# One decoder layer on one Trainium2 core: the mixer's groups reordered and taken off GpSimd, part of its low weights made earlier

## The chip, the cores and the metric

The kernel runs on one of the eight cores of a Trainium2 chip. A core has TensorE (PE in the profile; its weight loads are shown as PEld), VectorE (DVE), ScalarE (ACT), GpSimd (POOL), a queue engine for transfers (SyncE, SP) and 16 DMA engines. The metric is device time in microseconds (us). Before the change the median of three runs is 2429.63 us (2427.08 to 2433.99). A measurement of this kernel tells about 0.3%, some 7 us, from no change.

## The reference

The reference is one inference step of a hybrid decoder layer on 264 columns: 256 tokens of one prompt and 8 samples of one token each. All is float32.

```python
h += 0.5 * norm(swiglu_1(norm(h)))                      # 2048 -> 5632 -> 2048
u  = norm(h);  proj = u @ w_in                          # 2048 -> 10288
glu_a, glu_b, z, xBC, dt = split(proj)                  # 1024, 1024, 3072, 5120, 48
v  = silu(layernorm(causal_conv31(glu_a * sigmoid(glu_b))))
x, B, C = silu(causal_conv4(xBC))                       # 48 heads of 64, 8 groups of state 128
y  = ssd(x, softplus(dt), a, B, C) ; y = norm_of_group(y * silu(z))
h += norm(concat(v, y) @ w_out)
h += 0.5 * norm(swiglu_2(norm(h)))
h += norm(sigmoid(norm(h) @ w_gate) * (p @ w_proj))
```

For the prompt, `ssd` works in two chunks of 128 tokens: products of C and B masked and weighted with decays exp(a_i - a_j), times x, and a state carried from the first chunk to the second. For each sample it is one step: state times exp(dt a) plus the product of x dt and B, and y is that state times C. New convolution buffers and states are returned too.

## The kernel before

Activations lie with 128 features on the partitions and 264 columns beside each other. Every matrix product is made in three passes over split numbers: a weight is w = hi + lo and an activation x = (x0, x1), and `mm3` (L248) issues hi x0 (L250), hi x1 (L251) and lo x0 (L252). So each 128x128 weight tile costs three matmuls of 264 columns. One column block of the input projection ("a unit") has 16 such tiles, 48 matmuls.

Weights come through `Weights.load` (L138). A unit of up to 16 tiles is read in halves of 8 tiles, 512 KB each, into `wraw` (L153); ACT rounds a half to `whi` (L154), and DVE subtracts to give `wlo` (L155). Each of the three has four buffers, and loading runs two units ahead. The tables `PLAN` and `IN_ORDER` (L47) fix the order of the units.

The stages are: first feed-forward (44 gate and up pairs and 16 down columns in three chunks; L366 `ffn`), a small projection of p, then `u` for the mixer, made k by k (L534: DVE and POOL add the residual, DVE scales, ACT and DVE split) while PE already runs the first four columns of the input projection over the k that are ready. Then come the other 77 columns. For each of eight groups the order is B, C, x0, in four groups a GLU pair, x1, x2, z0, z1, z2; `dt` comes first of all, and the last four GLU pairs at the end.

Behind each column DVE and ACT do the short convolution (`do_conv`, L629: ACT scales, DVE adds three shifted terms, ACT takes SiLU). After x0, `decays` (L696) reads the prefix sums from memory into `ab` and `ea`, and ACT takes exponentials. After x2, `ssd` (L717) transposes x and B on PE (L727, L728), forms the decayed C B products, states and y. For the samples it writes the group's B and C to memory (`d_bc`, L785), reads C back spread over all partitions (`cbc`, L787), reads the three states in halves (`h0`, L792), multiplies them on POOL and sums them on DVE (L794). The gate of a group (`gate`, L809) runs behind x0 of the next group: y times silu(z) on DVE, squares on ACT, two additions on POOL into `run`, a matmul with ones (L306) that sums over partitions, and a scaling.

All transfers are issued by SP in one queue, in order: an issue that waits holds back those behind it. The instruction order on every engine is fixed when the program is built, by a scheduler; line numbers L216, L219, L243 are the helpers `tt`, `stt` and `act`, so groups are told apart by tile names.

Of the kernel before, what the change touches and what calls it, by code (L numbers as in the profile page):

```python
# [19 lines left out]
P = 128  # L20
# [93 lines left out]

_COLS = {}
# [12 lines left out]
class Weights:  # L128
# [4 lines left out]
    def __init__(self, tc, pool, w):  # L133
        self.tc, self.pool, self.w = tc, pool, w
        self.at = 0
        self.done = []

    def load(self, between=()):  # L138
# [5 lines left out]
        with nullcontext() if between else tc.high_priority(offset=1000):  # L144
            for a in range(0, n, 8):
# [8 lines left out]
                nc.scalar.copy(hi, raw)  # L154
                nc.vector.tensor_tensor(out=lo, in0=raw, in1=hi.bitcast(F32), op=ALU.subtract)  # L155
# [13 lines left out]
def kernel(ctx: ExitStack, tc: tile.TileContext, a: dict):  # L169
# [77 lines left out]

    def mm3(acc, wt, x, first, last):  # L248
# [3 lines left out]
        return nc.tensor.matmul(acc, lo, x[:, 0, :], start=False, stop=last).ins  # L252
# [76 lines left out]
    ws = Weights(tc, wpool, a["w"])  # L329
# [26 lines left out]
    def gemm_one(xs, kts, nunits=1):  # L356
        acc = acc_tile()
# [126 lines left out]
    bg.append(hist_mod)  # L484

# [48 lines left out]
    for k in range(KD + 2):  # L534
# [4 lines left out]
        if k >= 2:  # L539
            t = tmp()  # L540
            stt(t, H(k - 2), V("mix_pre", k - 2), r, ALU.mult, ALU.mult)
            us.append(split(t))
    ectx.close()
# [27 lines left out]
    def do_dt(acc):  # L571
# [21 lines left out]
        nc.sync.dma_start(d_dt[1], dta[:, NP_:])  # L593
# [6 lines left out]
        act(eap, eap, AF.Exp)  # L600
        pt = ps_tile([P, 2, 2, NH])
        for c in range(2):
            for i, s in ((0, dt), (1, dta)):
                nc.tensor.transpose(pt[:, c, i, :], s[:, P * c : P * c + P], ident[:NH, :NH])
        nc.scalar.copy(tm, pt)
        pc = ps_tile([P, 2, 2, NH])
        for c in range(2):
            nc.tensor.matmul(pc[:, 0, c, :], tri, tm[:, c, 1, :], start=True, stop=True)
            nc.tensor.matmul(pc[:, 1, c, :], ones, tm[:, c, 1, :], start=True, stop=True)
        nc.scalar.copy(acs, pc[:, 0])  # L610
        tt(dte, pc[:, 1], acs, ALU.subtract)
        act(dte, dte, AF.Exp)
        act(cd, pc[:, 1, 1, :], AF.Exp)
        pf = ps_tile([P, 2, P])
        for c in range(2):
            nc.tensor.matmul(pf[:NH, c, :], tm[:, c, 1, :], tri, start=True, stop=True)
        cs = tmp()[:NH]
        nc.scalar.copy(cs[:, :NP_].rearrange("h (c l) -> h c l", c=2), pf[:NH])
        nc.sync.dma_start(d_cs, cs[:, :NP_])
# [76 lines left out]
    def decays(g):  # L696

        hs = slice(HPG * g, HPG * g + HPG)
        ab = []
        for c in range(2):  # L700
            t = mp.tile([P, HPG, P], F32, tag="ab", bufs=2, name=nm("ab"))
            nc.sync.dma_start(t, d_cs[hs, P * c : P * c + P].partition_broadcast(P))
            for h in range(HPG):
                i = HPG * g + h
                act(t[:, h, :], t[:, h, :], AF.Relu, bias=acs[:, c, i : i + 1], scale=-1.0)
            act(t, t, AF.Exp, scale=-1.0)
            ab.append(t)
# [6 lines left out]
        act(ea, ea, AF.Exp)  # L714
        return ab, ea

    def ssd(g, bf, cf, xt, ab, ea):  # L717
# [5 lines left out]
        for c in range(2):  # L723
# [11 lines left out]
            b = mp.tile([P, P], F32, tag="btm", bufs=1, name=nm("btm"))  # L735
            nc.scalar.copy(b, pt[:, 3, :])
            btm.append(b)
        pcb = ps_tile([P, 2, P])
        for c in range(2):
            cols = slice(P * c, P * c + P)  # L740
            nc.tensor.matmul(pcb[:, c, :], bf[:, cols], cf[:, cols], start=True, stop=True)

        for c in range(2):
            cb = mp.tile([P, P], F32, tag="cb", bufs=1, name=nm("cb"))
            tt(cb, pcb[:, c, :], tri, ALU.mult)
            tt(ab[c], ab[c], cb.unsqueeze(1).to_broadcast([P, HPG, P]), ALU.mult)

        states = []
        for c in range(2):
# [7 lines left out]
            else:  # L757
                tt(s, states[0], cd[:, hs].unsqueeze(2).to_broadcast([P, HPG, 64]), ALU.mult, nc.gpsimd)
# [18 lines left out]
        tt(y[:, :, P:NP_], y[:, :, P:NP_], ea, ALU.add)  # L777

        js = slice(3 * g, 3 * g + 3)
        pr = ps_tile([P, 2, P])  # L780
        nc.tensor.transpose(pr[:NS, 0, :], bf[:, NP_:], ident)
        nc.tensor.transpose(pr[:NS, 1, :], cf[:, NP_:], ident)
        rows = mp.tile([P, 2, P], F32, tag="rows", bufs=1, name=nm("rows"))
        nc.scalar.copy(rows[:NS], pr[:NS])
        nc.sync.dma_start(d_bc[g].rearrange("i b n -> b i n"), rows[:NS])  # L785
        cbc = mp.tile([P, NS, P], F32, tag="cbc", bufs=1, name=nm("cbc"))
        nc.sync.dma_start(cbc, d_bc[g, 1].partition_broadcast(P))  # L787
        ych = mp.tile([P, 3, NS], F32, tag="ych", bufs=1, name=nm("ych"))
# [375 lines left out]
```

## Time and profile before

| what | value |
|---|---|
| median of three runs | 2429.63 us |
| profiled execution | 2432.44 us, span 2430.7 us |
| PE busy | 2367.7 us, 97% |
| DVE, ACT, POOL busy | 1569.2, 1181.4, 298.4 us |
| first feed-forward, steady part (100 to 700 us) | PE busy throughout, 182 GB/s |
| `u` and first four columns | about 775 to 815 us |
| rest of the input projection with all of the mixer | about 815 to 1360 us |
| output projection | about 1360 to 1545 us |
| second feed-forward, last stage | about 1545 to 2320 us, to the end |

PE is the engine that the whole kernel is built around, so time is read as time in which PE is not busy, or runs at a lower granted clock, and from the list of what PE waited for in each stretch. A wait of another engine matters only where PE waits for its result.

### The profile page before, as it was taken

What the parts mean: (1) busy time and instruction counts of PE and PEld (TensorE: products, weight loads), DVE (VectorE), ACT (ScalarE), POOL (GpSimd) and SP (SyncE); (2) the same over time, 40 slices, a digit from 0 to 9 for tenths busy, and PEclk for the clock granted to TensorE, in tenths of its full rate; (3) what the DMA queues carried; (4) which work ended last, traced back from release to release, by engine and by line L of the source; (5) the groups of instructions that cost most, each with busy time, mean ns of one, the idle gap of its engine ahead of it and who ended that gap; (6) DMA issues with size and microseconds to landing.
All of it is one profiled execution on the core that took longest, in us unless ns stands there. A gap on an engine that the chain in (4) does not pass through costs nothing.

```text
span 2430.7 us, 47409 instructions
## 1 busy us (share of the span) xinstructions
PE 2367.7 (97%) x19448; PEld 2342.7 (96%) x19448; DVE 1569.2 (65%) x2333; ACT 1181.4 (49%) x1771; POOL 298.4 (12%) x295
## 2 busy tenths in 40 slices
PE   8999999999999889999999999999999999999988
PEld 8999999999999889999999999999999999999988
DVE  6554455545557858988798975766545565565585
ACT  6444444433456465665565545544444443344465
POOL 0400000000015212122122010101000000000103
PEclk9999999999999999999999999999999999999999
DMA  7655555555556666666666556476766776676553
GB/s 249 217 183 184 182 183 182 183 183 183 183 169 207 213 180 193 207 216 202 210 216 205 181 181 216 153 238 228 240 213 223 237 236 217 217 236 206 184 191 132
DMA packets 166250, 489.89 MB, mean 202 GB/s; under 512 B 25568, under 2 KB 42640, under 8 KB 166032
## 3 DMA queue, kind: packets, MB, share of 16 engines
q1 hardware_dynamic: 166032, 486.86, 62.0%
q8 instruction: 152, 2.49, 0.4%
q14 instruction: 66, 0.54, 0.1%
HBM read 465.65 MB, written 22.42 MB: 201 GB/s over the span
## 4 chain that ended last, share of the span: by engine, by line
PE 84%; DVE 6%; issue 3%; ACT 3%; DMA 2%; POOL 1%; SPq 0%; ACTq 0%; POOLq 0%; DVEq 0%
PE acc L250 27%; PE acc L251 27%; PE acc L252 27%; DVE wlo L155 2%; DVE y L219 1%; ACT whi L154 1%; PE ps L306 1%; DVE h L216 1%; DMA ab<-d_cs 1%; DMA cbc<-d_bc 1%; DVE ych L794 1%; PE ps L250 0%; ACT tmp L243 0%; DMA d_bc<-rows 0%; PE ps L251 0%
## 5 line engine op out<-in xcount | busy, mean ns | idle before, releaser
L252 PE MATMUL acc<-act,wlo 128*128 128x264 f32 x6224 | 1770.7, 285 | 4.3 <-DVE wlo L155 4.1
L251 PE MATMUL acc<-act,whi 128*128 128x264 f32 x6224 | 1756.6, 283 | 6.3 <-DVE act L216 6.2
L250 PE MATMUL acc<-act,whi 128*128 128x264 f32 x6224 | 1747.7, 283 | 3.4 <-DVE tmp L216 2.1
L155 DVE TENSOR_TENSOR wlo<-wraw,whi 128x1024 fp32r<-128x1024 f32 (+2 forms) x812 | 986.9, 1217 | 597.9 <-ACT whi L154 595.5
L154 ACT CAST whi<-wraw 128x1024 fp32r<-128x1024 f32 (+2 forms) x812 | 829.9, 1026 | 961.9 <-PE acc L251 717.3
L250 PEld LDWEIGHTS acc<-act,whi 128*128 128x128 f32 x6224 | 1175.5, 190 | 6.0 <-issue 2.1
L251 PEld LDWEIGHTS acc<-act,whi 128*128 128x128 f32 x6224 | 1169.2, 188 | 9.9 <-DVE act L216 7.9
L252 PEld LDWEIGHTS acc<-act,wlo 128*128 128x128 f32 x6224 | 1167.9, 188 | 8.3 <-DVE wlo L155 6.4
L216 POOL TENSOR_TENSOR run<-run,tmp 128x264 f32<-128x264 f32 x93 | 87.8, 944 | 962.9 <-ACT tmp L243 961.8
L216 POOL TENSOR_TENSOR s<-s,eap 128x1024 f32<-128x1024 f32 x24 | 48.8, 2035 | 630.4 <-DMA s<-in_hst 630.4
L219 DVE SCALAR_TENSOR_TENSOR y<-v,vec,y 128x251 f32<-128x251 f32 (+23 forms) x240 | 118.1, 512 | 1.2
L219 DVE SCALAR_TENSOR_TENSOR s<-bb,xds,s 128x128 f32<-128x128 f32 x192 | 52.7, 346 | 66.1 <-POOL s L216 66.1
L216 POOL TENSOR_TENSOR h<-h,cbc 128x512 f32<-128x512 f32 x48 | 73.6, 1553 | 166.0 <-DMA cbc<-d_bc 90.9
L258 ACT CAST act<-tmp 128x264 fp32r<-128x264 f32 x120 | 48.7, 410 | 69.9 <-DVE tmp L216 55.2
L216 DVE TENSOR_TENSOR tmp<-acc,rr 128x264 f32<-128x264 f32 x100 | 43.0, 430 | 51.0 <-PE acc L252 50.8
L216 DVE TENSOR_TENSOR tmp<-tmp,acc 128x264 f32<-128x264 f32 x86 | 36.7, 427 | 38.7 <-PE acc L252 38.6
L216 DVE TENSOR_TENSOR act<-tmp,act 128x264 fp32r<-128x264 f32 x120 | 56.1, 471 | 0.3
L243 ACT ACTIVATE tmp<-tmp 128x264 f32<-128x264 f32 x112 | 47.0, 420 | 8.7 <-DVE tmp L216 8.4
L243 ACT ACTIVATE tmp<-y 128x264 f32<-128x264 f32 x67 | 28.0, 425 | 44.1 <-DVE y L216 43.0
L216 DVE TENSOR_TENSOR y<-y,acc 128x264 f32<-128x264 f32 x80 | 34.0, 425 | 24.0 <-PE acc L252 24.0
L794 DVE TENSOR_REDUCE ych<-h 128x4 f32<-128x512 f32 x48 | 32.4, 678 | 17.5 <-POOL h L216 17.5
L250 PE MATMUL ps<-act,whi 128*128 128x264 f32 x96 | 28.4, 304 | 15.4 <-ACT whi L154 8.1
(165 smaller groups left out, 926.1 us busy)
## 6 DMA issues: line engine op xcount, KB each, us to landing
wraw<-in_w SPq DMA_DIRECT2D x756, 512.0 KB, 4.7
h<-in_hst SPq DMA_DIRECT2D x48, 256.0 KB, 3.9
s<-in_hst SPq DMA_DIRECT2D x24, 512.0 KB, 6.5
out_nss<-s SPq DMA_DIRECT2D x24, 512.0 KB, 3.0
wraw<-in_w SPq DMA_DIRECT2D x24, 384.0 KB, 4.1
wraw<-in_w SPq DMA_DIRECT2D x32, 256.0 KB, 3.9
ab<-d_cs SPq DMA_DIRECT2D x16, 384.0 KB, 5.1
cbc<-d_bc SPq DMA_DIRECT2D x8, 512.0 KB, 4.3
```

What stands on the lines that cost most here:

```text
L154: nc.scalar.copy(hi, raw)
L155: nc.vector.tensor_tensor(out=lo, in0=raw, in1=hi.bitcast(F32), op=ALU.subtract)
L216: return (eng or nc.vector).tensor_tensor(out=out, in0=in0, in1=in1, op=op)
L219: return nc.vector.scalar_tensor_tensor(out=out, in0=in0, scalar=scalar, in1=in1, op0=op0, op1=op1)
L243: i = nc.scalar.activation(out=out, in_=in_, func=func, bias=bias, scale=scale)
L250: nc.tensor.matmul(acc, hi, x[:, 0, :], start=first, stop=False)
L251: nc.tensor.matmul(acc, hi, x[:, 1, :], start=False, stop=False)
L252: return nc.tensor.matmul(acc, lo, x[:, 0, :], start=False, stop=last).ins
L258: nc.scalar.copy(t[:, 0, :], x)
L306: nc.tensor.matmul(p, ones, s, start=i == 0, stop=i == len(self.parts) - 1)
L794: nc.vector.tensor_reduce(out=ych[:, j, b : b + 4], in_=h0, op=ALU.add, axis=AX.X)
```

## The change

**Order.** `IN_ORDER` puts the three z columns of group 0 behind dt, so that the first four columns are dt, z0, z1, z2 instead of dt, B, C, x0. C of a group now comes behind x2 of the group before it (C of group 0 behind the z), and z of groups 1 to 7 behind that.

**Low weights.** Of the 81 units of the input projection, 30 (the first four and then every third) are staged: during the first feed-forward, behind every second column, one half is read (`sraw`), rounded on ACT (`shi`), subtracted in place on DVE and written to a new memory tensor `low`. In the mixer these units still read `wraw` and make `whi`, but `wlo` is read from `low`. That is 60 loads, casts, subtractions and stores more in the first feed-forward, 60 subtractions fewer and 60 loads of 512 KB more later.

**Mixer.** POOL has no work in the groups: the product of state and C is made on DVE, whole states (512 KB) at a time, the state's decay (`st`) and the gate's two additions also. The product with C moves from behind x2 to behind x0, x1 and x2 (x1, x2 and the next C in the first two groups). The gate is cut in two: `gate_begin` behind B of the next group, `gate_end` behind its x0. The prefix sums and the decays are loaded earlier and used behind x1, and `decay_cb` (the C B products with the decays) also behind x1. `do_dt` is cut in parts. The exponential of the samples' decay is taken before its way through memory.

```diff
@@ the column order of the mixer's input projection
     for g in range(GRP):
+        z = [("z", MT_Z + 3 * g + j) for j in range(3)]
+        if g == 0:
+            out.extend(z)
+            out.append(("C", MT_CM))
         out.append(("B", MT_BM + g))
-        out.append(("C", MT_CM + g))
         out.append(("x", MT_X + 3 * g))
         if g in GLU_IN:
             pair()
         out.extend(("x", MT_X + 3 * g + j) for j in (1, 2))
-        out.extend(("z", MT_Z + 3 * g + j) for j in range(3))
+        if g + 1 < GRP:
+            out.append(("C", MT_CM + g + 1))
+        if g:
+            out.extend(z)
...
+def _staged():
+    ins = [i for i, u in enumerate(PLAN) if u[0] == "in"]
+    return ins[:4] + ins[5::3]
+STAGED = _staged()
@@ class Weights
+    def stage(self, pool, s, a):
+        tc, nc = self.tc, self.tc.nc
+        cols = slice(8 * P * a, 8 * P * (a + 1))
+        raw = pool.tile([P, 8 * P], F32, tag="sraw", bufs=3, name=f"sraw{s}_{a}")
+        hi = pool.tile([P, 8 * P], F32R, tag="shi", bufs=1, name=f"shi{s}_{a}")
+        with tc.issue_after(self.dma.ins):
+            nc.sync.dma_start(raw, self.w[STAGED[s], :, cols])
+        nc.scalar.copy(hi, raw)
+        lo = raw.bitcast(F32R)
+        nc.vector.tensor_tensor(out=lo, in0=raw, in1=hi.bitcast(F32), op=ALU.subtract)
+        with tc.issue_after(self.dma.ins):
+            nc.sync.dma_start(self.low[s, :, cols], raw)
...
                 self.dma = nc.sync.dma_start(raw, src[:, a : a + m, :])
-                nc.scalar.copy(hi, raw)
-                nc.vector.tensor_tensor(out=lo, in0=raw, in1=hi.bitcast(F32), op=ALU.subtract)
+                self.hi = nc.scalar.copy(hi, raw).ins
+                if i in STAGED:
+                    low = self.low[STAGED.index(i), :, a * P : (a + m) * P]
+                    nc.sync.dma_start(lo.bitcast(F32), low.rearrange("p (n c) -> p n c", n=m))
+                else:
+                    self.lo = nc.vector.tensor_tensor(
+                        out=lo, in0=raw, in1=hi.bitcast(F32), op=ALU.subtract
+                    ).ins
@@ gemm_one, and the first feed-forward
+        paced[0] += 1
+        if stage and paced[0] % 2:
+            stage.popleft()()
...
+    for i in range(len(STAGED)):
+        for half in range(2):
+            stage.append(lambda i=i, half=half: ws.stage(ep, i, half))
@@ the samples' state products
+    def to_memory(g, i, t):
+        pr = ps_tile([P, P])
+        nc.tensor.transpose(pr[:NS], t[:, NP_:], ident)
+        rows = mp.tile([P, P], F32, tag="rows", bufs=1, name=nm("rows"))
+        nc.scalar.copy(rows[:NS], pr[:NS])
+        nc.sync.dma_start(d_bc[g, i], rows[:NS])
...
+    def load_state(g, j):
+        h0s[g, j] = mp.tile([P, NS, P], F32, tag="h0", bufs=2, name=nm("h0"))
+        with tc.issue_after(ws.dma.ins):
+            nc.sync.dma_start(h0s[g, j], a["hst"][3 * g + j])
+    def state_times_c(g, j):
...
+        with tc.issue_after(ws.lo):
+            tt(h0, h0, cbcs[g], ALU.mult)
+            nc.vector.tensor_reduce(out=ychs[g][:, j, :], in_=h0, op=ALU.add, axis=AX.X)
...
-        for j in range(3):
-            for b in range(0, NS, 4):
-                h0 = mp.tile([P, 4, P], F32, tag="h0", bufs=3, name=nm("h0"))
-                nc.sync.dma_start(h0, a["hst"][3 * g + j][:, b : b + 4, :])
-                tt(h0, h0, cbc[:, b : b + 4, :], ALU.mult, nc.gpsimd)
-                nc.vector.tensor_reduce(out=ych[:, j, b : b + 4], in_=h0, op=ALU.add, axis=AX.X)
@@ the states and the gate
-                tt(s, states[0], cd[:, hs].unsqueeze(2).to_broadcast([P, HPG, 64]), ALU.mult, nc.gpsimd)
+                tt(s, states[0], cd[:, hs].unsqueeze(2).to_broadcast([P, HPG, 64]), ALU.mult)
...
-    def gate(g, y, zs):
+    def gate_begin(g, y, zs):
         tt(y, y, zs, ALU.mult)
-        sq = SumSq(3, direct=0)
+        sq = SumSq(3, direct=0, eng=nc.vector)
         for j in range(3):
             sq.add(y[:, j, :])
+        return g, y, sq
+    def gate_end(g, y, sq):
         t = tmp()
-        rsqrt(t, sq.total(), eps1, 1.0 / 384)
+        rsqrt(t, sq.total(traced[0]), eps1, 1.0 / 384)
@@ the loop over the columns
         elif kind == "B":
...
+            if g:
+                gated.append(gate_begin(g - 1, y, zs))
+                load_sums(g)
...
+            else:
+                do_sums(dt, dta)
+                load_cbc(0)
+            load_state(g, 0)
+            load_state(g, 1)
         elif kind == "C":
...
+            to_memory(g, 1, bcs[g, 1])
+            if 1 <= g <= 2:
+                state_times_c(g - 1, 2)
+                ssd_samples(g - 1, bcs[g - 1, 0], bcs[g - 1, 1], xt, y)
         elif kind == "x":
...
+            if j == 1:
+                if g == 0:
+                    do_exps(dta)
+                ab, ea = decays(g)
             do_conv(acc, m - MT_X, xt[:, j, :])
+            late = 0 if g > 1 else 1
+            if j >= late:
+                state_times_c(g, j - late)
...
+                if g:
+                    gate_end(*gated.pop())
```

The built order shows the staging on SP, in the first feed-forward, where every row before was a load into `wraw`. `wraw_0` and `wraw_8` are the two halves of a unit; now the rows are:

```order
L183 DMA wraw_0_1523<-in_w 128x1024
L183 DMA wraw_8_1529<-in_w 128x1024
L161 DMA sraw_0_1586<-in_w 128x1024
L183 DMA wraw_0_1593<-in_w 128x1024
L183 DMA wraw_8_1599<-in_w 128x1024
L166 DMA low<-sraw_0_1586 128x1024
L183 DMA wraw_0_1659<-in_w 128x1024
```

Behind two halves of weights stands a load of `sraw`, and its store to `low` behind the next two.

While `u` is made, DVE's order has these rows before (`tmp<-h` and `act` are the scaled and the split k tile, `tmp<-y` the residual):

```order
L219 SCALAR_TENSOR_TENSOR tmp_9279<-h_87,vec,rr_9018 128x264
L216 TENSOR_TENSOR act_9265<-tmp_9263,act_9265 128x264
L155 TENSOR_TENSOR wlo_0_9406<-wraw_0_9404,whi_0_9405 128x1024
L216 TENSOR_TENSOR act_9273<-tmp_9271,act_9273 128x264
L219 SCALAR_TENSOR_TENSOR tmp_9287<-h_87,vec,rr_9018 128x264
L216 TENSOR_TENSOR tmp_9292<-y_3338,rr_9000 128x264
L219 SCALAR_TENSOR_TENSOR tmp_9295<-h_88,vec,rr_9018 128x264
L216 TENSOR_TENSOR act_9281<-tmp_9279,act_9281 128x264
L155 TENSOR_TENSOR wlo_8_9412<-wraw_8_9410,whi_8_9411 128x1024
```

and now, over the same k tiles:

```order
L255 SCALAR_TENSOR_TENSOR tmp_9632<-h_88,vec,rr_9379 128x264
L252 TENSOR_TENSOR tmp_9637<-y_3327,rr_9361 128x264
L252 TENSOR_TENSOR act_9626<-tmp_9624,act_9626 128x264
L255 SCALAR_TENSOR_TENSOR tmp_9640<-h_88,vec,rr_9379 128x264
L252 TENSOR_TENSOR act_9634<-tmp_9632,act_9634 128x264
L255 SCALAR_TENSOR_TENSOR tmp_9648<-h_88,vec,rr_9379 128x264
L252 TENSOR_TENSOR tmp_9653<-y_3459,rr_9361 128x264
L252 TENSOR_TENSOR act_9642<-tmp_9640,act_9642 128x264
```

The subtractions into `wlo` have gone from between the k tiles; the residual's rows and the rest stand as before.

For the gate, POOL's order in the mixer was, in each group, the last of the states times C (`h<-h,cbc`), the two additions into `run`, and the next group's `st`:

```order
L216 TENSOR_TENSOR h_562_10737<-h_562_10737,cbc_10718 128x512
L216 TENSOR_TENSOR h_563_10741<-h_563_10741,cbc_10718 128x512
L216 TENSOR_TENSOR run_11173<-run_11173,tmp_11175 128x264
L216 TENSOR_TENSOR run_11173<-run_11173,tmp_11178 128x264
L216 TENSOR_TENSOR st_11538<-st_11532,cd 128x384
```

Now DVE has all of these. Around the gate of a later group its order is:

```order
L252 TENSOR_TENSOR h_12589<-h_12589,h_12798 128x792
L189 TENSOR_TENSOR wlo_8_12935<-wraw_8_12933,whi_8_12934 128x1024
L255 SCALAR_TENSOR_TENSOR b_12987<-acc_12926,vec,b_12987 128x255
L252 TENSOR_TENSOR b_12987<-b_12987,shist 128x8
L252 TENSOR_TENSOR run_12996<-run_12996,tmp_12998 128x264
L255 SCALAR_TENSOR_TENSOR b_12987<-acc_12926,vec,b_12987 128x254
L252 TENSOR_TENSOR run_12996<-run_12996,tmp_13001 128x264
L252 TENSOR_TENSOR h_706_13011<-h_706_13011,cbc_12800 128x1024
L255 SCALAR_TENSOR_TENSOR b_12987<-acc_12926,vec,b_12987 128x253
```

The first row is y times silu(z), the `b` rows are the convolution of B of the next group, and the last-but-one is a whole state times C. Both additions stand ahead of the convolution of x0, where POOL made them behind x0; the matmul with ones that waits for them on PE still stands in the unit behind x0 in most groups, and two to four units behind x0 in the first two.

More of the change, by code (lines that the diff above doesn't have):

```diff
@@ L251, in mm3 @@
         nc.tensor.matmul(acc, hi, x[:, 1, :], start=False, stop=False)
-        return nc.tensor.matmul(acc, lo, x[:, 0, :], start=False, stop=last).ins
+        traced[0] = nc.tensor.matmul(acc, lo, x[:, 0, :], start=False, stop=last).ins
+        return traced[0]
     def split(x, gain=None):
@@ L599, in do_dt @@
                 )
[L600 to L619, printed above, removed]
     def xo_piece(i):
@@ L694, in do_ln, with load_sums @@
             outk[i] = split(v)
[L696 removed]
+    sums = {}
+    def load_sums(g):
         hs = slice(HPG * g, HPG * g + HPG)
[L699 to L701 removed]
+        ab = [mp.tile([P, HPG, P], F32, tag="ab", bufs=2, name=nm("ab")) for _ in range(2)]
+        for c, t in enumerate(ab):
             nc.sync.dma_start(t, d_cs[hs, P * c : P * c + P].partition_broadcast(P))
[L703 to L707, printed above, removed]
         ea = mp.tile([P, 3, P], F32, tag="ea", bufs=1, name=nm("ea"))
@@ L734, in ssd @@
             xdt.append(t)
-            b = mp.tile([P, P], F32, tag="btm", bufs=1, name=nm("btm"))
+            b = rtile()[:, :P]
             nc.scalar.copy(b, pt[:, 3, :])
             btm.append(b)
[L738 to L746, printed above, removed]
         states = []
```

120 lines of the change are left out of this document (91 added, 29 removed).

## Prediction

> **What bounds the kernel now.** I read the page first, then the busy times by stretch, then what PE waited for.
>
> ```profile
> PE 2367.7 (97%) x19448; PEld 2342.7 (96%) x19448; DVE 1569.2 (65%) x2333; ACT 1181.4 (49%) x1771; POOL 298.4 (12%) x295
> ```
>
> PE is idle 63 us of 2430.7. The next view gives busy time (and instructions) of PE, PEld, DVE, ACT and POOL, the granted clock, the DMA share and GB/s.
>
> ```profile
> 100.00:700.00 600.00, 600.00 (x5002) 600.00 (x5001) 306.36 (x333) 246.67 (x299) 9.55 (x19) 1.00 0.58 182
> 775.00:815.00 40.00, 32.82 (x227) 30.33 (x228) 37.29 (x51) 22.96 (x47) 26.08 (x26) 0.96 0.75 253
> 845.00:905.00 60.00, 52.65 (x405) 49.98 (x404) 27.99 (x46) 36.16 (x72) 3.75 (x4) 0.94 0.58 167
> 905.00:930.00 25.00, 22.43 (x173) 22.11 (x172) 19.31 (x32) 13.41 (x24) 9.75 (x6) 0.93 0.73 238
> 930.00:1360.00 430.00, 415.09 (x3407) 400.76 (x3406) 372.10 (x643) 250.11 (x458) 86.40 (x66) 1.00 0.65 204
> 1560.00:2300.00 740.00, 739.55 (x6158) 739.17 (x6157) 432.62 (x647) 317.31 (x399) 57.14 (x35) 1.00 0.67 223
> ```
>
> In both feed-forwards PE never rests: 5002 matmuls in 600 us, 0.12 us each, so 5.76 us for a unit of 48. The change can gain only in 775 to 1360 us. What PE waited for between 760 and 1371 us, with times and the longest:
>
> ```profile
> PE ps L306 <- POOL run L216: 12.0, 9, 2.6
> PE ps L727 <- ACT h L243: 7.3, 2, 4.9
> PE acc L251 <- DVE act L216: 6.2, 7, 1.6
> PE acc L252 <- DVE wlo L155: 4.1, 8, 0.9
> PE ps L753 <- ACT btm L736: 1.1, 1, 1.1
> PE acc L250 <- ACT act L258: 0.9, 1, 0.9
> PE acc L250 <- DVE v L216: 0.4, 1, 0.4
> ```
>
> They sum to 32.0 us. The clock costs more: 0.04 of 40 us, 0.06 of 60 and 0.07 of 25 are 1.6 + 3.6 + 1.8 = 7.0 us. So 39 us is all there is to gain.
>
> **The change part by part.**
>
> **A, `u` (775 to 815).** PE is idle 7.2 us there and loses 1.6 us of clock, 8.8 in all, and DVE is busy 37.3 of 40.
>
> ```profile
> L155 DVE TENSOR_TENSOR wlo<-wraw,whi 128x1024 fp32r<-128x1024 f32 x10 | 14.5, 1462 | 0.5 <-ACT whi L154 0.5
> L216 POOL TENSOR_TENSOR h<-h,tmp 128x264 f32<-128x264 f32 x15 | 15.0, 1008 | 5.9 <-DVE tmp L216 5.6
> L216 POOL TENSOR_TENSOR tmp<-y,rr 128x264 f32<-128x264 f32 x7 | 8.0, 1148 | 3.1 <-DVE act L216 1.4 <-ACT rr L243 0.8 <-DMA wraw<-in_w 0.7
> ```
>
> All four units here are staged. Eight subtractions of 1.46 us go, 11.7 us of DVE, which leaves 25.6. POOL keeps 15.0 + 8.0 = 23.0 us, and PE needs 192 x 0.12 = 23.0: POOL is late next, but hardly later than PE. Gain 6 us, between 2 (POOL sets the pace) and 8.8.
>
> **B, the first group (845 to 905).** Idle 7.35 plus clock 3.6 is 10.9 us. The chain of waits shows why (start, us, what):
>
> ```profile
> 856.55 5.54 DMA d_cs<-tmp
> 862.11 3.98 DMA ab<-d_cs
> 866.17 1.49 ACT ab L243 x5
> ```
>
> The prefix sums go through memory, ACT waits to take exponentials, SiLU of x stands behind them, and PE's transposes wait. Counted in the built order, 50 matmuls lay between the prefix-sum matmul (L616) and the first transpose, 6 us; now 205 lie between it and the transposes of x1 and x2, 24.6 us. The same chain takes 5.5 + 4.0 and some 2 us for the copy and the issues, and then on ACT:
>
> ```profile
> L243 ACT ACTIVATE ab<-ab,acs 128x128 f32<-128x128 f32 x96 | 30.0, 390 | 15.8 <-DMA ab<-d_cs 15.8
> ...
> L243 ACT ACTIVATE ab<-ab 128x768 f32<-128x768 f32 x16 | 12.6, 831 | 0.0
> L238 ACT ACT_TABLE_LOAD x27 | 34.6, 1283 | 1.2 <-PEq L1123 0.8
> ```
>
> 12 x 0.39 + 2 x 0.83 + 1.28 and about 3.5 us of casts and evacuations that stand between: 11. Together 22.5 us, 2 us of room. But eight convolution columns now follow one another without a z column, so DVE is full. Gain 7 us, from 0 to 10.9.
>
> **C, the gate.** POOL's 12.0 us (11.8 behind 905) and the clock of 905 to 930, 1.8: 13.6.
>
> ```profile
> L216 POOL TENSOR_TENSOR run<-run,tmp 128x264 f32<-128x264 f32 x93 | 87.8, 944 | 962.9 <-ACT tmp L243 961.8
> L216 DVE TENSOR_TENSOR run<-run,tmp 128x264 f32<-128x264 f32 x42 | 18.0, 429 | 0.3
> ```
>
> Two additions take 0.86 us instead of 1.9, and they start behind B instead of behind x0, a unit of 5.76 us earlier for a matmul that has not moved. The longest wait was 2.6 us. Gain 11.5 us, up to 13.6, and 8 if two gates still wait 2.6 us.
>
> **D, DVE in the groups (905 to 1360: 391.4 of 455 us busy).** Waits of 4.1, 1.1 and 0.4 us.
>
> ```profile
> L155 DVE TENSOR_TENSOR wlo<-wraw,whi 128x1024 fp32r<-128x1024 f32 x133 | 170.0, 1282 | 28.3 <-ACT whi L154 27.4
> L216 POOL TENSOR_TENSOR h<-h,cbc 128x512 f32<-128x512 f32 x46 | 71.1, 1565 | 149.6 <-DMA cbc<-d_bc 74.6 <-DMA h<-in_hst 25.0 <-issue 17.6
> L794 DVE TENSOR_REDUCE ych<-h 128x4 f32<-128x512 f32 x47 | 31.7, 677 | 15.4 <-POOL h L216 15.4
> ...
> L155 DVE TENSOR_TENSOR wlo<-wraw,whi 128x1024 fp32r<-128x1024 f32 x246 | 300.7, 1224 | 202.9 <-ACT whi L154 202.5
> ```
>
> (The last row is the second feed-forward.) Behind the first four, 26 units are staged, 52 halves, some six of them before 905: 46 go, -59 us. Added: 24 products of 128x1024 at the subtraction's 1.224, 29.4; 16 additions of 0.43 and eight `st` of 384 columns, between 0.43 for 264 and 0.68 for 512, some 0.55; 11.3 together; the sums stay near 32. Net -18 us, from 86 to 82% busy. Gain 2.5 us of 5.6, from 0 to 5.6.
>
> The first and the last row also show what POOL costs DVE: 1282 ns beside POOL against 1224, 58 ns on 133 rows, 7.7 us. The Trainium skill (SBUF — State Buffer, "SBUF: two separate sides") says that a DVE operation with two SBUF inputs and a GpSimd operation lock a shared port pair, and that the loser blocks entirely. By that, an estimate: POOL's 96 us in 905 to 1360 would cost DVE up to 0.86 x 96 = 83 us, and D would reach its end, 3 us more. The trace bears out a part only: with 57 us of POOL in the second feed-forward the subtraction did not lengthen.
>
> **E, the loads of `wlo`.** Not shown before: PE waiting for a low weight from memory. A buffer is free when PE has left the half four earlier, so three halves, 8.6 us, remain to issue and land. The nearest landings are 4.6 us (weights, 100 to 700) and 6.5 (states, second feed-forward, median):
>
> ```profile
> wraw<-in_w SPq DMA_DIRECT2D x206, 512.0 KB, 4.6
> ...
> s<-in_hst SPq DMA_DIRECT2D x21, 512.0 KB, 6.5
> ```
>
> That leaves 2.1 to 4.0 us for SP. Its waits for other things, 905 to 1360:
>
> ```profile
> SPq L792 <- DVE ych L794: 45.4, 41, 3.1
> ...
> SPq L702 <- PE ps L768: 14.5, 6, 2.8
> SPq L639 <- ACT xo L634: 14.4, 7, 4.1
> ```
>
> Behind a waiting issue stand `wraw` and `wlo` of the next units, and PE behind those. These 74 us are 16% of the stretch; a load in one of them may be late by a microsecond or less. I take 4 us for 52 loads, between 0 and 52 (1 us each).
>
> **F, the staging (100 to 700).**
>
> ```profile
> L155 DVE TENSOR_TENSOR wlo<-wraw,whi 128x1024 fp32r<-128x1024 f32 (+1 forms) x209 | 256.0, 1225 | 236.2 <-ACT whi L154 236.0
> L154 ACT CAST whi<-wraw 128x1024 fp32r<-128x1024 f32 (+1 forms) x209 | 219.1, 1048 | 355.1 <-PE acc L251 242.5 <-issue 110.5 <-PE acc L252 2.1
> ```
>
> DVE waits for ACT and ACT for PE to leave a buffer: PE sets the pace. 60 casts of 1.05 and 60 subtractions of 1.22 over some 690 us raise ACT from 41 to 50% and DVE from 51 to 62%. 60 loads and 60 stores of 0.524 MB add 91 GB/s to 182. A raw half has from the low half four earlier to the next cast: 11.5 - 1.05 - 1.22 = 9.2 us for 4.6 of landing; behind that PE still holds three made halves. PE lost 0.45 of 740 us at 223 GB/s. Cost 0, at most 3.
>
> Sum: 6 + 7 + 11.5 + 2.5 - 4 = 23. The profiled execution took 2432.4 us (span 2430.7 and 1.7 around it), so it would take 2409; the median of the runs lies 2.8 us under it: **2407 us**.
>
> The Trainium skill (TensorE: Matmul & The Clock Gate, "Part 1: The HAM clock gate") lets the clock fall after an idle window of about 3.4 us. By that rule the dips at 775 and 905 should not be there (longest waits 1.6 and 2.6 us), and the gain would be 3.4 us smaller. The rows show both dips, so they stay in.
>
> **The rivals.**
>
> *All of it goes* (chance 0.14): every wait and dip ends and the loads are never late: 2429.6 - 39 = 2391. For it: the gate's long room. Against: POOL in A, and a full DVE in the first group.
>
> *The waits only change their cause* (0.13): DVE stays over 80% busy, so gate, states and convolutions wait for it instead of POOL, and PE for them; only A is left: 2424. For it: DVE is the busiest helper, and ACT waits for it in the groups. Against: PE's waits for DVE there were 4.5 us in all.
>
> *The low weights come late* (0.15): SP's one queue carries 52 more loads between issues that wait. A to D give 27 us, so the change loses from 27 / 52 = 0.52 us of mean lateness on. At 0.8 us it costs 42: 2445. For it: SP's waits of up to 4.1 us against 2.1 to 4.0 of room. Against: most weight issues wait for DVE's own pace, and DVE gets faster.
>
> **How the numbers follow.** Forecast 0.58, 2397 to 2420 by itself. A measurement of this kernel tells 0.3% (7.3 us) from no change. Faster: forecast and all of it, 0.72. Same: the second rival, 0.13. Slower: the third, 0.15. The range is 2391 to 2434: it leaves out most of the third rival and a little below.
>
> **What would show it.** A: no wait for `act` from 775 to 815, DVE well under 37 us. B: no wait of L833 for ACT near 860. C: no wait of L345. D: subtractions at 1.22 us. E: PE waiting for `low`. F: PE 600 of 600 in 100 to 700. The forecast is wrong if PE's waits in 760 to 1371 stay over 20 us, or if PE waits for the DMA by more than 10.

## The result: 0.8% slower

The changed kernel takes 2448.42 us (median of six runs, 2444.75 to 2457.3) against 2431.58 us for the kernel before on the same chip: a ratio of 1.0078, with a 95% interval of 1.0055 to 1.0100. The forecast was 2407 us, faster. The profiled execution shown here is the longest of the six (2457.3 us, span 2455.5), so its losses are some 9 us larger than those of the median.

The page of the changed kernel, busy time by engine:

```profile
PE 2381.4 (97%) x19448; PEld 2353.6 (96%) x19448; DVE 1565.5 (64%) x2357; ACT 1230.5 (50%) x1840; POOL 204.5 (8%) x223
```

Busy times by stretch of the changed kernel; the columns are those of the prediction. Everything behind the first feed-forward comes 25 to 36 us later than before, so the windows are shifted: the second is `u`, the third the first columns behind it, the fourth the first group, the fifth the other groups.

```profile
100.00:700.00 600.00, 588.99 (x4831) 583.84 (x4830) 335.90 (x371) 276.35 (x336) 21.09 (x38) 1.00 0.78 264
806.00:840.00 34.00, 31.64 (x233) 29.24 (x232) 28.91 (x43) 22.42 (x48) 22.59 (x26) 1.00 0.92 322
840.00:872.00 32.00, 26.61 (x195) 25.96 (x194) 16.83 (x27) 15.71 (x28) 2.92 (x4) 0.89 0.85 314
882.00:935.00 53.00, 46.01 (x369) 44.46 (x368) 32.48 (x54) 28.53 (x54) 0.00 (x0) 0.94 0.82 260
955.00:1385.00 430.00, 419.43 (x3451) 407.64 (x3451) 341.20 (x643) 253.68 (x467) 4.29 (x4) 1.00 0.78 256
```

The first row holds the surprise: 4831 matmuls in the 600 us in which there were 5002. At 0.12 us each, 171 matmuls are 20.5 us. (PE's busy time shows only 11 us of that, since the ends of matmuls are modelled; count instructions.) To find where time was lost I took the start of each of the 812 weight casts, which every kernel here has in the same order and which follow PE's progress. Behind the first feed-forward (cast 274) the changed kernel is 36 us late. At the end of the mixer (cast 450) it is 25 us late, and it stays so. So **the first feed-forward lost 36 us, and the mixer gained only 11 back** where the prediction had 0 and 23.

What PE waited for from 796 to 1396 us, the mixer of the changed kernel (total, times, longest):

```profile
PE acc L290 <- DMA wlo<-low: 14.2, 6, 7.0
PE ps L345 <- DVE run L252: 4.0, 4, 1.3
PE acc L288 <- ACT whi L184: 3.6, 1, 3.6
PE acc L289 <- DVE act L252: 1.2, 2, 1.0
PE acc L288 <- ACT h L279: 1.0, 1, 1.0
```

The old waits (12.0 for `run`, 7.3 for `h`, 6.2 for `act`, 4.1 for `wlo` from DVE) have gone or shrunk (`run` to 4.0), and low weights from memory have taken the first place. The clock adds to this: 0.89 of 32 us and 0.94 of 53 us in the rows above are 3.5 + 3.2 = 6.7 us, in two stretches of 6.8 us at half clock, one behind the wait of 3.6 us for `whi` and one behind the wait of 7.0 us for `wlo`.

### The profile page after: what moved, and what is told of

It is laid out like the page before. It is cut to its first block, busy times and chain, and to the rows that moved or that the text cites. A ratio compares the mean times of both kernels' runs of the same rounds, so it can differ in the third digit from the quotient of the medians.

```text
span 2455.5 us, 47685 instructions
## 1 busy us (share of the span) xinstructions
PE 2381.4 (97%) x19448; PEld 2353.6 (96%) x19448; DVE 1565.5 (64%) x2357; ACT 1230.5 (50%) x1840; POOL 204.5 (8%) x223
## 4 chain that ended last, share of the span: by engine, by line
PE 58%; DMA 5%; DVE 1%; ACT 1%; issue 1%; SPq 0%; DVEq 0%; ACTq 0%
PE acc L288 18%; PE acc L290 18%; PE acc L289 18%; DMA wlo<-low 2%; DMA d_bc<-rows 1%; DMA cbc<-d_bc 1%; PE ps L865 0%; DMA wraw<-in_w 0%; PE ps L850 0%; PE ps L288 0%; DVE wlo L189 0%; PE ps L289 0%; PE ps L290 0%; ACT whi L184 0%; PE ps L345 0%
## 5 line engine op out<-in xcount | busy, mean ns | idle before, releaser
L290 PE MATMUL acc<-act,wlo 128*128 128x264 f32 x6224 | 1774.8, 286 | 24.0 <-DMA wlo<-low 14.2
L189 DVE TENSOR_TENSOR wlo<-wraw,whi 128x1024 fp32r<-128x1024 f32 x752 | 901.1, 1203 | 394.4 <-ACT whi L184 378.4
L184 ACT CAST whi<-wraw 128x1024 fp32r<-128x1024 f32 (+2 forms) x812 | 820.4, 1024 | 641.1 <-PE acc L289 473.6
L164 DVE TENSOR_TENSOR sraw<-sraw,shi 128x1024 fp32r<-128x1024 f32 x60 | 73.6, 1226 | 268.2 <-ACT shi L162 268.2
L162 ACT CAST shi<-sraw 128x1024 fp32r<-128x1024 f32 x60 | 63.0, 1050 | 285.8 <-DMA sraw<-in_w 285.8
L252 POOL TENSOR_TENSOR run<-run,tmp 128x264 f32<-128x264 f32 x77 | 73.6, 957 | 921.1 <-ACT tmp L279 920.6
L255 DVE SCALAR_TENSOR_TENSOR y<-v,vec,y 128x255 f32<-128x255 f32 (+25 forms) x240 | 107.0, 470 | 2.0
L252 POOL TENSOR_TENSOR run<-run,y 128x264 f32<-128x264 f32 x7 | 8.7, 1237 | 584.3 <-ACT run L332 506.7
L252 DVE TENSOR_TENSOR h<-h,cbc 128x1024 f32<-128x1024 f32 x24 | 29.2, 1221 | 25.1 <-DMA cbc<-d_bc 19.9
```

The source lines that it names most:

```text
L184: self.hi = nc.scalar.copy(hi, raw).ins
L189: self.lo = nc.vector.tensor_tensor(out=lo, in0=raw, in1=hi.bitcast(F32), op=ALU.subtract).ins
L252: return (eng or nc.vector).tensor_tensor(out=out, in0=in0, in1=in1, op=op)
L255: return nc.vector.scalar_tensor_tensor(out=out, in0=in0, scalar=scalar, in1=in1, op0=op0, op1=op1)
L290: traced[0] = nc.tensor.matmul(acc, lo, x[:, 0, :], start=False, stop=last).ins
```

## The first feed-forward: what the staging stalls

The groups of the staging in 100 to 700 us:

```profile
L164 DVE TENSOR_TENSOR sraw<-sraw,shi 128x1024 fp32r<-128x1024 f32 x50 | 61.3, 1225 | 244.6 <-ACT shi L162 244.6
L162 ACT CAST shi<-sraw 128x1024 fp32r<-128x1024 f32 x50 | 52.5, 1050 | 260.2 <-DMA sraw<-in_w 260.2
```

The work costs what was forecast, 1.05 and 1.225 us. But ACT stands still 260 us in front of its 50 casts, and DVE 245 us in front of its subtractions. ACT's timeline shows what stands behind (start, us, the idle time before in brackets):

```profile
461.00 1.05 ACT L162 CAST shi<-sraw 128x1024 fp32r<-128x1024 f32 x1 [6.42 <-DMA sraw<-in_w]
461.95 1.99 ACT L184 CAST whi<-wraw 128x1024 fp32r<-128x1024 f32 x2
...
474.44 1.05 ACT L162 CAST shi<-sraw 128x1024 fp32r<-128x1024 f32 x1 [6.20 <-DMA sraw<-in_w]
475.39 1.99 ACT L184 CAST whi<-wraw 128x1024 fp32r<-128x1024 f32 x2
...
487.49 1.05 ACT L162 CAST shi<-sraw 128x1024 fp32r<-128x1024 f32 x1 [5.82 <-DMA sraw<-in_w]
```

And SP's timeline of the same stretch (start, us from the first issue's begin to the last one's end):

```profile
463.33 0.33 SPq L166 DMA_DIRECT2D low<-sraw  x1
464.47 1.80 SPq L183 DMA_DIRECT2D wraw<-in_w  x2
466.32 1.33 SPq L161 DMA_DIRECT2D sraw<-in_w  x1
...
476.78 0.33 SPq L166 DMA_DIRECT2D low<-sraw  x1
477.91 1.80 SPq L183 DMA_DIRECT2D wraw<-in_w  x2
479.76 0.43 SPq L161 DMA_DIRECT2D sraw<-in_w  x1
```

Read them as one round; two more weight halves, loaded behind the staged one, belong to it (their rows on SP are left out). The staged load is issued at 479.76, behind two weight loads, and is there at 487.49, 7.7 us later. On ACT its cast stands *ahead* of the casts of those two weight halves, so they wait for it, and DVE's subtractions with them. The store (SP waits for it) and the next weight loads (whose buffers these subtractions free) come behind, and then the next staged load. This round of 13.0 us (474.44 to 487.49) stages one half while PE has work for two units, 11.5 us. Over the 600 us there are 50 casts, so the mean round takes 12.0 us, and PE, which needs 11.5, waits for the rest. There were three suspects: the amount of work (DMA 264 GB/s for 182, casts, subtractions), the store that SP waits at, and the place of the cast on ACT.

**A load one step ahead, and the cast later.**

Here `self.hi` is the last weight cast issued so far.

```diff
             with tc.issue_after(self.dma.ins):
                 nc.sync.dma_start(raw, self.w[STAGED[s], :, cols])
+            self.loaded.append((raw, s, cols))
+        if len(self.loaded) > 1 or s == len(STAGED):
+            raw, s, cols = self.loaded.popleft()
...
-            nc.scalar.copy(hi, raw)
+            with tc.issue_after(self.hi):
+                nc.scalar.copy(hi, raw)
```

> Staging as in the change, but each staged half is loaded one staging step before it is cast and stored, and its cast stands behind the weight casts already due. Theory (a closed loop: the store waits on SP for a subtraction that waits for the cast that waits for the load just issued, 13.4 us a half where PE needs 11.5 for its two units): the 36 us that the first feed-forward lost come back, all but 0 to 5; ACT waits for sraw under 20 us instead of 286; time 2412 to 2418 us, ratio to the kernel before 0.992 to 0.995. Rival (the work itself is too much: DMA at 264 instead of 182 GB/s, 60 casts and 60 subtractions more): bytes, casts and subtractions are the same here, so the loss stays, ratio 1.005 to 1.010.

Measured: 2420.75 us, ratio 0.9954 (0.9936 to 0.9971), a little above the range given. The first feed-forward:

```profile
100.00:700.00 600.00, 600.00 (x5003) 600.00 (x5002) 365.86 (x385) 296.10 (x350) 15.27 (x26) 1.00 0.82 274
```

5003 matmuls, and none lost, at 274 GB/s, more than the changed kernel moved. Only at the end of the first feed-forward (weight cast 274) is this run 2.5 us behind the kernel before, where the changed kernel was 36. So the amount of work is cleared but for these 2.5 us.

**Only the stores moved.** The same code without the condition on the cast:

```diff
-            with tc.issue_after(self.hi):
-                nc.scalar.copy(hi, raw)
+            nc.scalar.copy(hi, raw)
```

As built, the scheduler puts the casts back to where the change has them on ACT (two neighbouring pairs apart), and what is left of the edit is that each store is issued behind the next staged load.

> Only the stores move: the store of a staged half is issued behind the load of the next one, four weight loads later. The cast keeps its place on ACT, ahead of two weight casts, and still waits there for a load just issued. Theory (SP closes the loop): without SP in it the wait on ACT is shorter than the 8.6 us of made weights that PE holds; ratio 0.992 to 0.998, ACT still waits for sraw over 150 us in all. Rival one (the wait on ACT ahead of the weight casts is enough by itself): ratio 1.003 to 1.008. Rival two (the amount of work): 1.005 to 1.010.

Measured: 2497.19 us, ratio 1.0273 (1.0254 to 1.0293). My theory fell: with the store out of the round it turned out slower, not faster. ACT waits 331 us for `sraw`. What is left of the round goes through the weight buffers, as the waits of SP in 20 to 770 us suggest (an issue of `wraw` waits for a buffer; a row names the DVE instruction whose end released it):

```profile
SPq L188 <- DVE tmp L257: 314.7, 74, 9.3
SPq L188 <- DVE wlo L194: 154.9, 94, 8.4
```

SP waits for buffers in an undisturbed run too, but not for 9.3 and 8.4 us at a time: with the casts moved (next run) a wait for `wlo` lasts 3.4 us at most. Why this run is worse than the change's own order is only argued: four weight loads, the staged load and a store now go out together, and the median landing of `sraw` is 7.2 us, where it was 5.8.

**Only the casts moved.** One line added to the change.

```diff
-        nc.scalar.copy(hi, raw)
+        with tc.issue_after(self.hi):
+            nc.scalar.copy(hi, raw)
```

> The change with one addition: the cast of a staged half is held on ACT behind the two weight casts whose loads were issued ahead of it, and no longer stands in front of them. SP issues in the order of the run with the stores apart, which was at 1.027. Theory (ACT in its order waits for the load just issued, weight casts and the subtractions that free the raw buffers stand behind, and the next loads behind those): PE is busy 600 of 600 us from 100 to 700, ratio 0.993 to 0.998. Rival (a load a whole step ahead is needed, or the stores on SP hold up the weights): PE loses 15 us or more there, ratio 1.000 to 1.027.

Measured: 2417.63 us, ratio 0.9953 (0.9938 to 0.9968). In the instructions as built, SP's are the same, one by one, as in the run with the stores apart (the scheduler moves the stores along); what differs is the place of the casts on ACT, two weight casts later, and of the subtractions that follow them. The group of casts from 100 to 700 us, and the stretch:

```profile
L163 ACT CAST shi<-sraw 128x1024 fp32r<-128x1024 f32 x53 | 55.4, 1046 | 0.0
```

```profile
100.00:700.00 600.00, 600.00 (x5003) 600.00 (x5002) 365.94 (x386) 296.09 (x350) 15.29 (x26) 1.00 0.83 274
```

No wait is left in front of them, though the staged loads do not land sooner (median 7.5 us). Sixty casts, two places each, are worth 78 us between these two runs (1.0273 to 0.9953, of 2430), and some 30 us against the change (1.0078 to 0.9953). The first rival named for the run with the stores apart, the wait on ACT ahead of the weights, was the cause. This run, too, is 2.5 us behind the kernel before at cast 274.

## The mixer: which part brings what

**Nothing staged**: the new order, and no GpSimd in the groups.

```diff
-    return ins[:4] + ins[5::3]
+    return []
```

> The new order and the move from GpSimd alone: no unit is staged, all 81 low weights are subtracted in place. Theory: the first feed-forward is as before (the loss of 36 us was the staging's), the waits for low weights from memory (14.2 us and a clock dip of 3.4) are gone, and the order keeps some 29 us less 3 for u and some 10 for a DVE that is now over 85% busy in the groups: 2416 us (2408 to 2426), ratio 0.990 to 0.998. Rival (without the staged weights DVE binds the groups and PE waits for it instead of for GpSimd): 2427 to 2436, ratio 0.998 to 1.002.

Measured: 2408.48 us, ratio 0.9911 (0.9895 to 0.9928), at the good end. PE waits for DVE in the mixer by 6.4 us (`act`) and 3.8 us (`wlo`), so DVE does not take GpSimd's place.

**Four units staged**, the change's own way:

```diff
-    return ins[:4] + ins[5::3]
+    return ins[:4]
```

> Only the first four input units are staged, 8 halves instead of 60, in the change's own way. Theory: 8 trips of the loop and the gap at 52 us cost some 8 us in the first feed-forward, none of the waits for low weights behind the first units remain, u keeps its gain of about 6: 2420 us (2412 to 2430), ratio 0.992 to 0.999, and the cost in the first feed-forward is in proportion to the staged halves, 5 to 10 us. Rival (a fixed cost, or one of the DMA's total): a loss in the first feed-forward of under 2 or over 20 us.

Measured: 2410.32 us, ratio 0.9927 (0.9901 to 0.9953). The time is a little under the range given. The cost in the first feed-forward was 1.1 us in the profiled execution, not 5 to 10, so the proportion that I expected is not there. But the runs spread over 12 us, and this was the fastest of them. In the profiled execution of the change the same eight rounds cost 8.1 us (up to cast 50): its first staged half was there 1.6 us later (cast at 49.95 us instead of 48.35), and PE's gap there was 3.2 us with half clock behind it instead of 1.7 us without. So what eight rounds cost in this way is somewhere between 1 and 8 us.

**The same four, cast in the right place** (the load a step ahead as above):

> Only the first four input units staged, each half loaded a step ahead and cast behind the weight casts. Theory: what 8 halves still cost in the first feed-forward (1.1 us at the end of it) goes, the mixer is that of the run with the first four: 2404 to 2409 us, ratio 0.989 to 0.992, 8 to 18 us under the run with all 30 staged in this way. Rival (the other 26 units are worth having once they are staged for nothing): 2416 or more.

Measured: 2404.97 us (2404.56 to 2405.92), ratio 0.9900 (0.9885 to 0.9915). This is the best kernel of the study, 1.0% under the kernel before. Its mixer waits, 765 to 1390 us:

```profile
PE acc L294 <- ACT whi L190: 4.3, 1, 4.3
PE acc L296 <- DVE wlo L195: 3.5, 4, 1.3
PE ps L840 <- ACT h L285: 2.8, 1, 2.8
...
PE ps L351 <- DVE run L258: 1.1, 1, 1.1
```

So A to D together bring 24.7 us, and the other 26 units take 13 to 16 us of that back (2417.63 and 2420.75 against 2404.97). The 2.5 us at the end of the first feed-forward are part of this (the best kernel is 0.1 us behind there); the other 10 to 13 us are lost in the mixer. Why they are is the next question.

**D alone: no subtraction, no load** for the 26 units (`BARE`); the third matmul takes the high weight.

```diff
-                if i in STAGED:
+                if i in BARE:
+                    lo = hi
+                elif i in STAGED:
```

> The first four staged as in the change; for the other 26 units the subtraction is left out and nothing is loaded for it: the third matmul takes the high weight again, so the output lacks their low part. This is what the 26 staged units can bring in the mixer at most. Theory (DVE at 80 to 90% is no bound: PE waits for it under 5 us there): 2404 to 2410 us, ratio 0.989 to 0.993, within 5 us of the run with the first four alone. Rival (DVE binds the groups): 2402 or less, 8 us or more under that run.

Measured: 2403.88 us, ratio 0.9895 (0.9880 to 0.9910). Against the best kernel (0.9900) the intervals overlap: taking 52 subtractions from DVE brings about 1 us, which is not clear of noise, since PE hardly waited for DVE. (The four units are staged here in the change's own way, which cost the run with the first four 1.1 us; so it may be 2 us.) There was next to nothing for the 26 units to win.

**E: another queue** for the low weights, on the run with the loads ahead:

```diff
-                    nc.sync.dma_start(lo.bitcast(F32), low.rearrange("p (n c) -> p n c", n=m))
+                    nc.gpsimd.dma_start(lo.bitcast(F32), low.rearrange("p (n c) -> p n c", n=m))
```

> All 30 staged for nothing as in the run with the loads ahead, and the loads of low weights issued by GpSimd's queue instead of SP's. Theory (they are late because SP issues them in order, behind weights and behind issues that wait): PE waits under 3 us for low weights instead of 10.0, ratio 0.990 to 0.994. Rival (they are late because memory takes 6.6 us and more to land them, at 260 GB/s and over): PE still waits 7 us or more for them, ratio 0.994 to 1.000.

Measured: 2425.95 us, ratio 0.9984 (0.9969 to 0.9999): no better, rather 5 us worse (the intervals just touch). Yet the first half of the theory came true. Its mixer waits, 770 to 1400 us:

```profile
PE ps L840 <- ACT h L285: 6.1, 6, 2.7
PE acc L294 <- ACT whi L190: 4.5, 1, 4.5
PE acc L296 <- DVE wlo L195: 4.1, 4, 2.8
...
PE acc L296 <- DMA wlo<-low: 1.8, 1, 1.8
```

With the loads ahead and SP issuing the low weights, the first wait was:

```profile
PE acc L296 <- DMA wlo<-low: 10.0, 5, 3.7
```

The wait for low weights fell from 10.0 to 1.8 us, and much of it came back under other names: 6.1 for `h` instead of 1.0, 4.1 instead of 0.7 for `wlo` from DVE. Something behind all of them is late.

**The traffic by itself**: the best kernel, and two copies of 512 KB from memory to memory for each of the 26 units, which nobody reads or waits for.

```diff
+                if i in IDLE:
+                    to = self.idle[IDLE.index(i), :, a * P : (a + m) * P]
+                    with tc.issue_after(self.dma.ins):
+                        nc.sync.dma_start(to.rearrange("p (n c) -> p n c", n=m), src[:, a : a + m, :])
```

> The run with the first four staged ahead, all other subtractions in place, and beside each of the 26 units that the change stages later two copies of 0.5 MB from memory to memory that nobody reads: the traffic of the low weights without anyone who waits for it. Theory (the 26 units cost the mixer through memory: weights landed in 6.3 us instead of 4.8, states in 6.6 instead of 5.1, C in more, and DVE waits for C and the states): half or more of the 13 to 16 us between the two runs comes back as a loss: 2411 to 2421 us, ratio 0.992 to 0.996, and landings of weights of 5.6 us and more. Rival (SP's order: each low load stands behind a weight load that waits for DVE, and PE waits for the low weight itself): 2408 or less.

Measured: 2423.81 us, ratio 0.9972 (0.9960 to 0.9983): over the range given, and 18.8 us slower than the best kernel, none of it lost in the first feed-forward. The 26 units lost 10 to 13 us behind it. So traffic that nobody waits for is enough by itself. The copies are not quite the same load: a copy also writes to memory, it is issued in SP's queue, and DVE keeps its subtractions. (The share of the DMA engines in 930 to 1360 us is 0.78 at 256 GB/s, as with the staged units, 0.78 at 259.) PE now waits, in 770 to 1400 us, above all for low weights that DVE makes late:

```profile
PE acc L301 <- DVE wlo L196: 16.3, 8, 4.2
```

How the traffic gets there is seen in two views of 905 to 1360 us. Median landings in the best kernel, and then in the run with the loads ahead (the profile gives no landing of weights for the idle copies):

```profile
wraw<-in_w SPq DMA_DIRECT2D x141, 512.0 KB, 4.8
h<-in_hst SPq DMA_DIRECT2D x18, 512.0 KB, 5.1
```

```profile
wraw<-in_w SPq DMA_DIRECT2D x139, 512.0 KB, 6.3
wlo<-low SPq DMA_DIRECT2D x44, 512.0 KB, 6.6
h<-in_hst SPq DMA_DIRECT2D x19, 512.0 KB, 6.6
```

The weights landed in 6.0 us, too, when the low weights came through GpSimd's queue. So it is not their place in SP's queue that holds the others up, but the traffic.

How long DVE waited for C, in the best kernel, with the loads ahead, and with the idle copies:

```profile
DVE h L258 <- DMA cbc<-d_bc: 7.7, 4, 3.1
```

```profile
DVE h L258 <- DMA cbc<-d_bc: 18.6, 6, 4.9
```

```profile
DVE h L263 <- DMA cbc<-d_bc: 23.2, 7, 5.8
```

And the chain of waits ahead of a late low weight, with the loads ahead (start, us, what):

```profile
1015.31 4.28 DMA d_bc<-rows
...
1019.61 4.34 DMA cbc<-d_bc
...
1027.92 1.14 DVE wlo L195
...
1029.50 7.18 DMA wlo<-low
```

C goes to memory and back, DVE waits for it with a subtraction behind, the subtraction frees a weight buffer, SP issues that weight and then the low one behind it, and this takes 7.2 us to land. Three landings stand in this one chain. C's way back took 4.3 us in it; the one landing of it that the best kernel's profile gives took 3.6. That the lengthenings add up along such chains is argued from this one; no run changed one landing alone.

## The gate

**The additions back on GpSimd**, at their new place, in the best kernel; and **on VectorE at their old place**, in the kernel before.

```diff
-        sq = SumSq(3, direct=0, eng=nc.vector)
+        sq = SumSq(3, direct=0)
```

The second edit is the same line the other way round.

> The run with the first four staged ahead, but the two additions of squares of each gate are back on GpSimd, at their new place behind B. Theory (the place gives the room: a whole unit of 5.76 us more, against 1.9 us for two additions on GpSimd): PE waits for run under 3 us, 2405 to 2409 us, ratio 0.989 to 0.992. Rival (the engine is what made the gate late): PE waits for run 8 to 12 us again, 2412 to 2417 us, ratio 0.993 to 0.996.

> The kernel before with one word: the two additions of squares of each gate run on VectorE, at their old place; nothing staged, old order. Theory (the place): DVE is busy with other work there, PE goes on waiting for run by 6 us or more, 2425 to 2431 us, ratio 0.998 to 1.001. Rival (the engine): the 12.0 us of waits fall under 4, 2418 to 2423 us, ratio 0.995 to 0.997. Both runs near their second number would say that either half of the edit is enough by itself only if this one falls and the other stays.

Measured: 2406.67 us, ratio 0.9902 (0.9887 to 0.9917), and 2424.25 us, ratio 0.9980 (0.9970 to 0.9989). The waits for `run` in the first and in the second:

```profile
PE ps L351 <- POOL run L258: 1.9, 4, 0.8
```

```profile
PE ps L306 <- DVE run L216: 8.4, 8, 1.9
```

Of 12.0 us of waits the new place leaves 1.9, the other engine alone 8.4. The theory held: most of it is the unit of room. GpSimd at that place costs 1.7 us, with intervals that overlap. The other engine alone is worth some 5 us of time (its interval ends below 1).

The place was tried only in the new kernel, where GpSimd has no other work in the groups. In the kernel before that other work did not hold the additions up, as GpSimd's row for 905 to 1360 us shows: it stood idle in front of them until ACT's squares came.

```profile
L216 POOL TENSOR_TENSOR run<-run,tmp 128x264 f32<-128x264 f32 x16 | 16.2, 1013 | 72.9 <-ACT tmp L243 72.3
```

## Why the prediction was wrong

**F, the staging: the step that failed.** Forecast "Cost 0, at most 3"; measured some 30 us (0.0125 of 2430), which one line on the place of the cast takes away. The step counted work and room for each stream by itself (casts 1.05, subtractions 1.22, 9.2 us of room for a landing of 4.6). The work was right, and the room was enough: with the cast moved, weights landed in 5.6 us instead of 4.6, and 274 GB/s and a DVE busy 61% of the time cost 2.5 us, within the range. It left out **what stands behind the waiting instruction on its engine**: the built order of ACT had `shi` ahead of two weight casts whose loads were issued ahead of its own, and the slack was reckoned as if only the staging would wait. The Trainium skill says it in a sentence (PSUM — Partial Sum Buffer, "Engine vs sequencer instructions"): the queues of ScalarE, VectorE and GpSimdE are strict FIFO (first in, first out); the 260 us of ACT agree. Within the 36 us of the profiled run two single stalls count for more than their length: gaps of 3.2 us at 52.6 and 4.9 us at 734 between matmuls, each followed by 6.8 us at half clock, together some 15 us. The term had no part for the clock.

**E, the low loads: right in its mechanism by half, mis-sized.** Forecast 4 us, between 0 and 52; measured 10 to 13 in the mixer. PE waits for `low` by 10 to 14 us as the rival said, and the chain above has SP's queue in it. But the queue was not the price: freed from it, the time did not fall, and traffic without any waiting cost as much and more. The prediction priced only the lateness of the low weights themselves, with landings from stretches of 182 and 223 GB/s (4.6 and 6.5 us); it had no term for what 25% more traffic does to every other landing (weights from 4.8 to 6.3 us).

**A to D: right.** Forecast 27 us together, measured 24.7 in the best kernel. The four parts of this are estimates from single profiles. A was 6, and is 3.5 (2408.48 against 2404.97, with intervals that overlap); a wait of 4.3 us for `whi` takes the place of that for `act`, and whether the order of ACT there or a memory at 400 GB/s sets it was not tried. B was 7 of 10.9: from 845 to 905 us the best kernel has 57.17 of 60 us at a clock of 0.97, a loss of 4.6, so 6.3 came; what is left there is the wait of 2.8 us of PE's transposes for ACT (`h`, in the rows of the best kernel) and a stretch at half clock behind it. C was 11.5: waits from 12.0 to 1.3 and the clock of 905 to 930 back at 1.00, some 12.5. D was 2.5: about 1 from the subtractions; they take 1218 ns with GpSimd out, as expected.

The prediction says that the trace bears out only a part of the blocking between DVE and GpSimd, from a mean of 1282 ns. Instruction by instruction, the trace of the kernel before shows more. In 905 to 1360 us, 119 of 132 subtractions take 1.21 to 1.26 us. The other 13 all began while GpSimd was in an instruction, and took up to 2.31 us: one that began 0.08 us into a GpSimd instruction of 1.30 us took 2.30. Where a subtraction began first, it kept its 1.21 us, and GpSimd's product beside it took up to 2.4 us instead of 1.3. So one of the two does wait for the other, and the mean hides it because few meet: 8 us in all for the subtractions.

**The balance.** The forecast of 2407 us missed 2448 by 41. Some 30 of these are F, some 9 to 12 are the 26 units (13 to 16 with their part of the first feed-forward, for a forecast of 4), and 2 are A to D.

**The rivals.** The third had the right sign, but for the smaller half: low weights coming late would have left a gain of some 10 us. The slower result came from a wait that none of the rivals named. The signs given for F and E did show it (589 of 600 us; 14.2 us of waits for `low`, over the 10 named). The sign for C was not clean in the changed kernel (4.0 us of waits at L345).

## What to carry to other kernels

Work put into idle time of an engine in order is free only if it does not wait there ahead of work that others need: look at what its instruction waits for and which critical instructions stand behind it, and place it behind those, or load its input a step earlier. Price added traffic by the landings that it lengthens in chains that go through memory, not by the bandwidth that is left. Before relieving an engine, see whether anyone waits for it.

## What the runs showed that was not expected

- Sixty casts, each two places later on ACT, decided between a ratio of 1.0273 and 0.9953, with SP's instructions the same.
- Landings lengthen far from saturation: weights took 4.8 us at 211 GB/s (DMA share 0.64) and 6.3 at 259 (0.78). In the feed-forward 274 GB/s cost 2.5 us; that no chain there goes through memory twice may be why, which was not tried.
- With the four units staged, the DMA engines ran at 350 to 440 GB/s from 792 to 812 us (in slices of 0.7 us), and low weights took 10.2 us to land. The Trainium skill (Perfetto Trace Analysis, "Roofline") gives about 435 GB/s for one core's 16 DMA engines; the trace agrees.
- GpSimd issues a load in 0.54 us of its own time, and the low weights then land in 7.5 us, against 6.6 from SP's queue.
